# Gated DeltaNet in a fused decoder trunk: decay by selecting products, transposed A and attention, heads as a stair

## The chip, the cores and the metric

The kernel runs on one core of one Trainium2 chip. The metric is the device time of one execution in microseconds (us). TensorE (PE) multiplies matrices into PSUM, VectorE (DVE), ScalarE (ACT) and GpSimd (POOL) work on elements, and SyncE (SP) issues DMAs. Each engine takes its own instructions strictly in their order.

## What is computed

Two layers over 256 tokens with 1024 channels: a retention mixer with a SwiGLU, then a gated DeltaNet mixer with a SwiGLU, RMSNorm ahead of each and at the end. The change touches the DeltaNet mixer alone. It has 16 value heads and 8 key heads of 128 channels. The reference computes it in chunks of 64 tokens; both kernels use two chunks of 128, which is the same function.

```python
def rmsnorm(x, gain):
    xf = x.astype(jnp.float32)
    y = xf * lax.rsqrt(jnp.mean(xf * xf, axis=-1, keepdims=True) + NORM_EPS)
    return (y * gain.astype(jnp.float32)).astype(x.dtype)
...
def gated_delta_chunked(q, k, v, g, beta):
    """Gated delta rule S_t = a_t (I - b_t k_t k_t^T) S_{t-1} + b_t k_t v_t^T, o_t = S_t^T q_t."""
    ...
    gcum = jnp.cumsum(gc, axis=-1)
    ...
    decay_mat = jnp.where(causal, jnp.exp(gdiff), 0.0)
    k_beta = kc * bc[..., None]
    a_mat = jnp.where(strict, jnp.einsum('bhncd,bhnmd->bhncm', k_beta, kc) * decay_mat, 0.0)
    lhs = a_mat + jnp.eye(c, dtype=jnp.float32)
    rhs = jnp.concatenate([vc * bc[..., None], k_beta * jnp.exp(gcum)[..., None]], axis=-1)
    sol = lax.linalg.triangular_solve(lhs, rhs, left_side=True, lower=True, unit_diagonal=True)
    ...
    attn = jnp.where(causal, jnp.einsum('bhncd,bhnmd->bhncm', qc, kc) * decay_mat, 0.0)
    q_dec = qc * jnp.exp(gcum)[..., None]
    ...
    def step(state, xs):
        ui, wi, qi, ki, ai, gl = xs
        v_new = ui - jnp.einsum('bhcd,bhdv->bhcv', wi, state)
        o = jnp.einsum('bhcd,bhdv->bhcv', qi, state) + jnp.einsum('bhcm,bhmv->bhcv', ai, v_new)
        state = state * jnp.exp(gl)[..., None, None] + jnp.einsum('bhcd,bhcv->bhdv', ki, v_new)
        return state, o
...
def gdn_mixer(hdn, w_in, conv_w, a_log, dt_bias, norm_gain, w_out):
    proj = hdn @ w_in
    ...
    qkv = jax.nn.silu(causal_depthwise_conv(qkv, conv_w))
    ...
    beta = jax.nn.sigmoid(beta_logit.astype(jnp.float32))
    g = -jnp.exp(a_log.astype(jnp.float32)) * jax.nn.softplus(
        a.astype(jnp.float32) + dt_bias.astype(jnp.float32))
    o = gated_delta_chunked(q, k, v, g, beta)
    o = o * lax.rsqrt(jnp.mean(o * o, axis=-1, keepdims=True) + NORM_EPS) * norm_gain.astype(jnp.float32)
    o = o.reshape(b, s, GDN_V) * jax.nn.silu(z.astype(jnp.float32))
    return o.astype(hdn.dtype) @ w_out

def reference(x, positions, ...):
    h = x
    for i in range(DEPTH):
        ...
        h = h + mix          # retention for i = 0, gated DeltaNet for i = 1
        h = h + swiglu(rmsnorm(h, norm_ffn[i]), ffn_w_in[i], ffn_w_out[i])
    return rmsnorm(h, norm_final)
```

## The kernel before

All products with weights go through slabs of 128x1024 elements: SP loads raw, ScalarE casts whi (line 131), VectorE subtracts wlo (line 133), TensorE multiplies three times, high by high, high by low and low by high (lines 139 to 141). raw, whi and wlo have three buffers each. The projections use four PSUM banks (pool mm), everything else on TensorE four others (pool ip, tiles ip and tp).

The layer is a list of jobs, one for each slab (gdn, from line 1016). Beside them run generators, spawned by the jobs and moved on by one step after each job. From this a scheduler makes the order of every engine; the order is fixed in the built kernel.

- gates (line 641) makes beta and the log decay g, and by decay (line 718) the matrix D for each chunk and head: VectorE and GpSimd multiply a strict triangle by g (line 699, in a high and a low part gmh and gml), TensorE sums it with the triangle Ur (line 722), ScalarE takes the exponential of 512 columns, four heads at once (line 723).
- taps (line 725) is the convolution over four tokens of a projected slab in PSUM: one ScalarE and three VectorE instructions (line 732) for each half, then a silu on ScalarE.
- amat (line 754) makes A, the keys' products with beta and D: chunk 0 on VectorE (line 786), chunk 1 on ScalarE and GpSimd (lines 781, 782). invert (line 792) sends A to memory and back as Ab, so that all 32x32 diagonal blocks lie in partitions, inverts them by 31 pairs of VectorE instructions pr and Vb (lines 821, 823), sends the result to memory and back as Vd and Vc (lines 828, 831), transposes it (Tc, line 841), and merges blocks to 64 and to 128 by TensorE products and ScalarE copies (lines 857 to 891), one chunk after the other.
- attn (line 895): products of queries and keys, a ScalarE copy kq, a GpSimd product with D (line 925), four transposes for each (line 200), a ScalarE copy back into D.
- inner (line 935) is done for each group hg of four heads, once the inverse and the attention are there: solve (line 946), du (line 968), the products with the state (line 960) and with the attention (line 954), the norm and the gate with z; then yh and yl, the input of the output projection w_out (line 331).

The input projection's slabs come in the order z0 k q z1 v0 z2 v1 v2 v3 z3. In w_out the first six slabs of one half of the columns come, then six of the other half.

## Time and profile before

| | |
|---|---|
| median of 3 runs | 869.85 us (869.81 to 870.68) |
| the profiled execution | 869.91 us, of which its span is 868.1 us |
| granted TensorE clock | 0.997 of full speed |
| busy in the span | PE 842.7 us (97%), DVE 555.1 (64%), ACT 451.2 (52%), POOL 57.1 (7%) |
| chain of work that ended last | PE 80%, DVE 11%, the rest 9% |

The DeltaNet layer lies between about 400 and 675 us of the span. A timeline row gives the start and the length of a stretch of equal instructions; TensorE's matmuls overlap, so what one costs is read from start to start, and the idle time that a row names is a little less than what the queue lost. VectorE's instructions overlap by some 0.08 us too.

### The profile page before, as it was taken

Reading aid. Unit: us, or ns where it says so; the run is one execution under the profiler, and the core shown is the slowest. Engines: PE = TensorE matmul, PEld = TensorE weight load, DVE = VectorE, ACT = ScalarE, POOL = GpSimd, SP = SyncE. Lnnn points to the kernel's source line nnn. Section 1 sums busy time; section 2 is a strip of 40 time slices with the busy share of each in tenths; the row PEclk is TensorE's granted clock in tenths of the full one; section 3 lists DMA queues with packets and bytes.
Section 4 is the critical chain, followed back from the end, with each engine's and each line's share of the span. In section 5 each row is a group of like instructions: output and inputs, shape, how many; then the busy total and the mean of one; then the engine's idle time right before and its main releaser. Section 6 shows DMA issues by size and latency. Waiting matters only on the chain.

```text
span 868.1 us, 12759 instructions
## 1 busy us (share of the span) xinstructions
PE 842.7 (97%) x4917; PEld 718.6 (83%) x4917; DVE 555.1 (64%) x829; ACT 451.2 (52%) x770; POOL 57.1 (7%) x56
## 2 busy tenths in 40 slices
PE   8999999999999999999999988999899999999996
PEld 7789987888888889886998877989788888889885
DVE  4787877655555555454889899854665555555453
ACT  4553235554444444344687745687845544444343
POOL 0000000000000000000217141000200000000000
PEclk9999999999999999999999999999999999999998
DMA  8576445556556555554554734732045656555552
GB/s 262 186 208 173 123 146 165 174 193 197 189 179 189 184 183 174 189 191 122 146 147 127 214 99 137 191 135 73 4 167 169 210 180 193 180 183 182 183 193 74
DMA packets 121902, 143.54 MB, mean 165 GB/s; under 512 B 14145, under 2 KB 67954, under 8 KB 121842
## 3 DMA queue, kind: packets, MB, share of 16 engines
q1 hardware_dynamic: 121666, 142.66, 52.9%
q8 instruction: 38, 0.62, 0.3%
q14 instruction: 22, 0.18, 0.1%
q10 hardware_dynamic: 144, 0.07, 0.0%
q0 software_dynamic: 32, 0.01, 0.0%
HBM read 140.62 MB, written 2.10 MB: 164 GB/s over the span
## 4 chain that ended last, share of the span: by engine, by line
PE 80%; DVE 11%; issue 3%; DMA 3%; ACT 3%; POOL 1%; SPq 0%; POOLq 0%; ACTq 0%; DVEq 0%
PE mm L140 24%; PE mm L141 24%; PE mm L139 24%; DVE wlo L133 3%; PE tp L200 3%; DVE cacc L732 2%; DVE pr L821 2%; DVE Vb L823 1%; PE ip L960 1%; DMA raw<-gdn_w_in 1%; PE ip L552 1%; ACT junk L992 1%; DMA h<-x 1%; PE ip L946 1%; PE ip L544 1%
## 5 line engine op out<-in xcount | busy, mean ns | idle before, releaser
L133 DVE TENSOR_TENSOR wlo<-raw,whi 128x1024 fp32r<-128x1024 f32 x260 | 319.6, 1230 | 232.3 <-ACT whi L131 230.3
L131 ACT CAST whi<-raw 128x1024 fp32r<-128x1024 f32 x260 | 273.2, 1052 | 303.3 <-PE mm L140 225.2
L139 PE MATMUL mm<-whi,xh 128*128 128x512 f32 (+1 forms) x576 | 220.0, 385 | 1.2 <-ACT xh L636 0.7
L140 PE MATMUL mm<-whi,xl 128*128 128x512 f32 (+1 forms) x576 | 219.7, 382 | 0.5 <-DVE xl L315 0.3
L141 PE MATMUL mm<-wlo,xh 128*128 128x512 f32 (+1 forms) x576 | 208.0, 382 | 1.2 <-DVE wlo L133 1.2
L141 PEld LDWEIGHTS mm<-wlo,xh 128*128 128x128 f32 x576 | 108.5, 189 | 22.5 <-DVE wlo L133 2.6
L139 PEld LDWEIGHTS mm<-whi,xh 128*128 128x128 f32 x576 | 108.9, 189 | 21.1 <-ACT whi L131 1.0
L140 PEld LDWEIGHTS mm<-whi,xl 128*128 128x128 f32 x576 | 108.9, 189 | 21.0 <-issue 0.7
L139 PE MATMUL mm<-xh,whi 128*128 128x256 f32 x384 | 111.1, 289 | 0.0
L140 PE MATMUL mm<-xh,wlo 128*128 128x256 f32 x384 | 109.6, 285 | 1.2 <-DVE wlo L133 1.2
L141 PE MATMUL mm<-xl,whi 128*128 128x256 f32 x384 | 109.1, 284 | 0.0
L140 PEld LDWEIGHTS mm<-xh,wlo 128*128 128x128 f32 x384 | 73.4, 191 | 3.3 <-DVE wlo L133 1.8
L139 PEld LDWEIGHTS mm<-xh,whi 128*128 128x128 f32 x384 | 73.4, 191 | 1.3 <-issue 0.5
L141 PEld LDWEIGHTS mm<-xl,whi 128*128 128x128 f32 x384 | 73.4, 191 | 0.3
L139 PE MATMUL mm<-whi,hh 128*128 128x512 f32 x176 | 69.8, 397 | 0.0
L140 PE MATMUL mm<-whi,hl 128*128 128x512 f32 x176 | 69.6, 396 | 0.0
L141 PE MATMUL mm<-wlo,hh 128*128 128x512 f32 x176 | 64.3, 396 | 0.0
L732 DVE SCALAR_TENSOR_TENSOR cacc<-mm,conv,cacc 128x253 f32<-128x253 f32 (+2 forms) x96 | 45.6, 510 | 8.0 <-ACT cacc L729 7.4
L139 PE MATMUL mm<-whi,yh 128*128 128x512 f32 x128 | 49.5, 394 | 1.0 <-ACT yh L314 1.0
L140 PE MATMUL mm<-whi,yl 128*128 128x512 f32 x128 | 50.4, 394 | 0.0
L141 PE MATMUL mm<-wlo,yh 128*128 128x512 f32 x128 | 49.2, 397 | 0.0
L141 PEld LDWEIGHTS mm<-wlo,hh 128*128 128x128 f32 x176 | 33.1, 188 | 8.1
(235 smaller groups left out, 876.8 us busy)
## 6 DMA issues: line engine op xcount, KB each, us to landing
raw<-ffn_w_in SPq DMA_DIRECT2D x88, 512.0 KB, 3.5
raw<-ret_w_in SPq DMA_DIRECT2D x48, 512.0 KB, 4.0
raw<-gdn_w_in SPq DMA_DIRECT2D x48, 512.0 KB, 4.0
raw<-ffn_w_out SPq DMA_DIRECT2D x44, 512.0 KB, 3.6
raw<-ret_w_out SPq DMA_DIRECT2D x16, 512.0 KB, 3.3
raw<-gdn_w_out SPq DMA_DIRECT2D x16, 512.0 KB, 3.6
h<-x SPq DMA_DIRECT2D x4, 256.0 KB, 6.4
out<-o SPq DMA_DIRECT2D x4, 256.0 KB, 2.3
```

What stands on the lines that cost most here:

```text
L131: nc.scalar.copy(hi, raw)
L133: lo_ = nc.vector.tensor_tensor(lo, raw, hi.bitcast(F32), ALU.subtract)
L139: t.matmul(out, lh, rh, start=first, stop=False)
L140: t.matmul(out, ll, rh, start=False, stop=False)
L141: self.last_mm = t.matmul(out, lh, rl, start=False, stop=last).ins
L200: self.nc.tensor.transpose(out, in_, self.ident[:n, :n])
L544: nc.tensor.matmul(sp[:, c0:c0 + S - i0], k[:, d, j * P:(j + 1) * P], q[:, d, i0:S], start=d == 0, stop=d == 1)
L552: nc.tensor.matmul(op, sT[:, t * P:(t + 1) * P], b["v"][0][:, h], start=True, stop=t == 0)
L732: self.nc.vector.scalar_tensor_tensor(acc[:, s:S], ps[:, 0:S - s], cw[:, i, blk:blk + 1], acc[:, s:S], ALU.mult, ALU.add)
L821: V.tensor_tensor(tmp, Vb[:, 0:n, i:i + 1].broadcast_to([P, n, m]), Ab[:, n:32, i].unsqueeze(1).broadcast_to([P, n, m]), ALU.mult)
L823: V.tensor_tensor(Vb[:, 0:n, n:32], Vb[:, 0:n, n:32], tmp, ALU.subtract)
L946: T.matmul(up[:, j], b["V"][c][:, 4 * hg + j], v[c][:, j], start=True, stop=True)
```

## The change

- Decay: the running sum of g is transposed (gcT). For each group of heads and chunk one product writes "never" (-1e30 above the diagonal) into a PSUM bank, and for each head a product of 32 rows selects that head's row of gcT and adds it (tile_position). An exponential for each head, with the negative running sum as its bias, makes D, now transposed and with exact zeros, so the selections on GpSimd go.
- A is made transposed, both chunks by VectorE from PSUM. The squares of the norms replace one of the two scalings by beta: v is scaled by the key's norm kn, and uu is multiplied by beta2 on VectorE.
- The attention is one VectorE product from PSUM into D; copies, GpSimd products and transposes go.
- The merges use the transposed A, and each step is written for both chunks in a row. Tc comes ahead of the copies into Vf.
- inner of group hg starts when group hg-1 has taken two steps. The slabs come in the order z0 k q z1 z2 z3 v0 v1 v2 v3, and w_out changes between its halves after every two slabs up to the sixth.

```diff
-    def out_proj(self, w, yT, nk, nxt, early=None):
+    def out_proj(self, w, yT, nk, nxt, early=()):
...
-        p0 = self.proj_tok(w, 0, 512, yT, nk, None, (early,) if early else (), (), first)
-        p1 = self.proj_tok(w, 512, 512, yT, nk, None, (early,) if early else (), (last,), second)
+        p0 = self.proj_tok(w, 0, 512, yT, nk, None, early, (), first)
+        p1 = self.proj_tok(w, 512, 512, yT, nk, None, early, (last,), second)
...
+        gp = self.psip()
+        T.matmul(gp[:, 0:P], g4.rearrange("p r x -> p (r x)"), Uc, start=True, stop=True)
+        gcT = self.t1("gcT", (P,))
+        V.tensor_copy(gcT, gp[:, 0:P])
...
         b["D"] = [self.big(f"D{c}") for c in range(NT)]
-        pend = []
-        for c in range(NT):
-            for hg in range(4):
-                hs = slice(hg * 4, hg * 4 + 4)
-                gm = [self.t2(n, dt=F32R) for n in ("gmh", "gml")]
-                for eng, x, y in zip((V, V if hg % 2 else G), gm, (gh.bitcast(F32), gl)):
-                    eng.tensor_tensor(x, slb, y[:, c, hs].unsqueeze(2).broadcast_to([P, 4, P]), ALU.mult)
-                pend.append((c, hs, gm))
-                if len(pend) == 3:
-                    self.decay(b, Ur, *pend.pop(0))
...
-        for x in pend:
-            self.decay(b, Ur, *x)
+        never, eye = self.t1("never", (P,), F32R), self.t1("eye", (P,), F32R)
+        V.tensor_scalar(never, self.SL, -1e30, None, ALU.mult)
+        V.tensor_copy(eye, self.ident)
+        for hg in range(4):
+            dp = [self.psip().rearrange("p (h i) -> p h i", h=4) for _ in range(NT)]
+            for x in dp:
+                T.matmul(x, eye, never.unsqueeze(1).broadcast_to([P, 4, P]), start=True, stop=False)
+            for j in range(4):
+                for c in range(NT):
+                    q = 2 * (hg % 2) + c
+                    r, n = slice(32 * q, 32 * q + 32), 32 * q + c * NH + 4 * hg + j
+                    T.matmul(dp[c][:, j], self.ident[r, n:n + 1].broadcast_to([32, P]), gcT[r], start=False, stop=j == 3,
+                             tile_position=(32 * q, 0))
+            for c in range(NT):
+                for j in range(4):
+                    h = 4 * hg + j
+                    b["exp"] = A_.activation(b["D"][c][:, h], dp[c][:, j], AF.Exp,
+                                             bias=negc[:, c * NH + h:c * NH + h + 1]).ins
+            yield
         b["decayed"] = True
-
-    def decay(self, b, Ur, c, hs, gm):
-        dp = self.psip()
-        for i, x in enumerate(gm):
-            self.nc.tensor.matmul(dp, Ur, x.rearrange("p h j -> p (h j)"), start=i == 0, stop=i == 1)
-        b["exp"] = self.nc.scalar.activation(b["D"][c][:, hs].rearrange("p h j -> p (h j)"), dp, AF.Exp).ins
...
-        V.tensor_scalar(rk, b["kss"][:, :, ks], EPS, None, ALU.add)
-        G.tensor_tensor(rk, rk, self.mhalf[:, 0:4].rearrange("p (t h) -> p t h", t=NT), ALU.pow)
...
+        V.tensor_scalar(k2, b["kss"][:, :, ks], EPS, None, ALU.add)
+        G.tensor_tensor(rk, k2, self.mhalf[:, 0:4].rearrange("p (t h) -> p t h", t=NT), ALU.pow)
...
+        V.tensor_tensor(b["kn"][:, :, ks], k2, rk, ALU.mult)
+        V.tensor_tensor(rk, rk, rk, ALU.mult)
...
+        V.tensor_tensor(w2(beta2), w2(b["beta"]), rk.unsqueeze(3).broadcast_to([P, NT, 2, 2]), ALU.mult)
...
-            if c >= 1:
-                kk = self.t2("kk")
-                for j in range(4):
-                    h = 4 * sl + j
-                    A_.activation(kk[:, j], pp[:, j // 2], AF.Copy, scale=beta2[:, c, h:h + 1])
-                G.tensor_tensor(b["A"][c][:, 4 * sl:4 * sl + 4], kk, b["D"][c][:, 4 * sl:4 * sl + 4], ALU.mult)
-                continue
             for j in range(4):
                 h = 4 * sl + j
                 V.scalar_tensor_tensor(b["A"][c][:, h], pp[:, j // 2], beta2[:, c, h:h + 1], b["D"][c][:, h],
...
-        for c in range(NT):
-            for hg in range(4):
-                dm = b["D"][c][:, hg * 4:hg * 4 + 4]
-                G.affine_select(dm, dm, [[0, 4], [-1, P]], ALU.is_ge, 0.0, base=0, channel_multiplier=1)
...
-                            Ab[:, n:32, i].unsqueeze(1).broadcast_to([P, n, m]), ALU.mult)
+                            Ab[:, i, n:32].unsqueeze(1).broadcast_to([P, n, m]), ALU.mult)
             V.tensor_tensor(Vb[:, 0:n, n:32], Vb[:, 0:n, n:32], tmp, ALU.subtract)
...
-        yield
-        yield
+        for _ in range(4):
+            yield
+        V.transpose(Tc.rearrange("p a b -> p (a b)"), Vc.rearrange("p a b -> p (a b)"))
         for c in range(NT):
             for q in range(4):
                 qs = slice(32 * q, 32 * q + 32)
                 V.tensor_copy(Vf[c][qs, :, qs], Vc[qs, c * NH:(c + 1) * NH, :])
-        V.transpose(Tc.rearrange("p a b -> p (a b)"), Vc.rearrange("p a b -> p (a b)"))
...
         for c in range(NT):
             hs = slice(c * NH, (c + 1) * NH)
+            X.append(self.t2("X", (NH, 32)))
             xp = [h32(self.psip()) for _ in blocks]
             for h in range(NH):
                 for (q, b0, b1), x in zip(blocks, xp):
-                    T.matmul(x[b0, h], Am[c][b1, h, b0], Vc[b1, c * NH + h], start=True, stop=True,
-                             tile_position=(32 * q + 32, 32 * q))
+                    T.matmul(x[b1, h], Am[c][b0, h, b1], Tc[b0, c * NH + h], start=True, stop=True,
+                             tile_position=(32 * q, 32 * q + 32))
             for (q, b0, b1), x in zip(blocks, xp):
-                A_.copy(X[b0], x[b0])
-            yield
+                A_.copy(X[c][b1], x[b1])
...
+        yield
+        for c in range(NT):
             vp = [h32(self.psip()) for _ in blocks]
             for h in range(NH):
                 for (q, b0, b1), x in zip(blocks, vp):
-                    T.matmul(x[b0, h], Tc[b0, c * NH + h], X[b0, h], start=True, stop=True,
-                             tile_position=(32 * q, 32 * q))
+                    T.matmul(x[b0, h], X[c][b1, h], Vc[b1, c * NH + h], start=True, stop=True,
+                             tile_position=(32 * q + 32, 32 * q))
...
-        pend = None
         for c in range(NT):
             cs = slice(c * P, (c + 1) * P)
             for hp in range(4):
-                at = self.t2("att")
                 pp = self.psip().rearrange("p (x j) -> p x j", j=P)
                 for j in range(2):
-                    T.matmul(pp[:, j], b["qT"][:, 2 * hp + j, cs], b["kT"][:, 2 * hp + j, cs], start=True, stop=True)
-                kq = self.t2("kq", (2, P))
-                nc.scalar.copy(kq, pp[:, 0:2])
-                G.tensor_tensor(at.rearrange("p (j w) x -> p j w x", w=2),
-                                b["D"][c][:, 4 * hp:4 * hp + 4].rearrange("p (j w) x -> p j w x", w=2),
-                                kq.unsqueeze(2).broadcast_to([P, 2, 2, P]), ALU.mult)
-                if pend:
-                    flush(*pend)
-                pend = (c, hp, at)
+                    T.matmul(pp[:, j], b["kT"][:, 2 * hp + j, cs], b["qT"][:, 2 * hp + j, cs], start=True, stop=True)
+                dv = b["D"][c][:, 4 * hp:4 * hp + 4].rearrange("p (j w) x -> p j w x", w=2)
+                V.tensor_tensor(dv, pp[:, 0:2].unsqueeze(2).broadcast_to([P, 2, 2, P]), dv, ALU.mult)
                 yield
-        flush(*pend)
         b["attended"] = True
...
+        yield
+
+        while not (b.get("inverted") and b.get("attended") and (hg == 0 or b["steps"].get(hg - 1, 0) >= 2)):
+            yield
+        for _ in self.chunks(b, hg, v):
+            b["steps"][hg] = b["steps"].get(hg, 0) + 1
+            yield
+
+    def chunks(self, b, hg, v):
...
             uu = self.t2("uu")
-            A_.copy(f4(uu), f4(up))
+            V.tensor_tensor(uu, up, b["beta2"][:, c, hs].unsqueeze(2).broadcast_to([P, 4, P]), ALU.mult)
...
-            V.scalar_tensor_tensor(v[1][:, j], kp[:, j], b["beg"][:, 4 * hg + j:4 * hg + j + 1], v[1][:, j],
+            V.scalar_tensor_tensor(v[1][:, j], kp[:, j], b["nege"][:, 4 * hg + j:4 * hg + j + 1], v[1][:, j],
...
             for t in range(NT):
-                for j in range(2):
-                    h = 4 * hg + 2 * sl + j
-                    A_.activation(v[t][:, 2 * sl + j], tp[:, j, t], AF.Copy, scale=b["beta1"][:, t, h:h + 1])
+                h = 2 * hg + sl
+                A_.activation(v[t][:, 2 * sl:2 * sl + 2], tp[:, :, t], AF.Copy, scale=b["kn"][:, t, h:h + 1])
...
-        for group in "z0 k q z1 v0 z2 v1 v2 v3 z3".split():
+        for group in "z0 k q z1 z2 z3 v0 v1 v2 v3".split():
...
-        self.out_proj(w_out, yT, 16, nxt, early=6)
+        self.out_proj(w_out, yT, 16, nxt, early=(2, 4, 6))
```

Three places show what the scheduler makes of it. TensorE, decay, before: gmh and gml are the two parts of the products with g, Ur the triangle, mm the projection of k beside it.

```order
L722 MATMUL ip_3656<-gmh_3605,Ur_3520 128x512
L141 MATMUL mm_3799<-xl_3339,whi_3778 128x256
L139 MATMUL mm_3799<-xh_3338,whi_3778 128x256
L140 MATMUL mm_3799<-xh_3338,wlo_3779 128x256
...
L722 MATMUL ip_3656<-gml_3606,Ur_3520 128x512
...
L722 MATMUL ip_3700<-gmh_3644,Ur_3520 128x512
L722 MATMUL ip_3700<-gml_3645,Ur_3520 128x512
```

The same place after; never and eye are the constant and its unit matrix, gcT the transposed running sum, cst the constants' tile that selects.

```order
L711 MATMUL ip_3522<-never_3518,eye_3519 128x512
L711 MATMUL ip_3523<-never_3518,eye_3519 128x512
L716 MATMUL ip_3522<-gcT_3498,cst_75 128x128
L716 MATMUL ip_3523<-gcT_3498,cst_75 128x128
...
L711 MATMUL ip_3566<-never_3518,eye_3519 128x512
L716 MATMUL ip_3566<-gcT_3498,cst_75 128x128 x4
L140 MATMUL mm_3847<-xh_3338,wlo_3766 128x256
```

Two products of 512 columns for each bank, spread among the projection, have become one of 512 and four of 128 in a block; the selecting ones alternate between two banks in one part (c of 0 and 1 at different rows), and go four at a time to one bank in another.

ScalarE after, in the middle of the v slabs; zs3 is the silu of the last z group from its banks mm_4696 and mm_4697, vc and cacc the convolution of v. Before, z3 was the last group and stood behind all v slabs.

```order
L131 CAST whi_5449<-raw_5448 128x1024
L738 ACTIVATE vc_5255<-cacc_5262 128x256
L730 ACTIVATE cacc_5387<-mm_5321,conv_86 128x256
L131 CAST whi_5509<-raw_5508 128x1024
L1038 ACTIVATE zs3_3423<-mm_4696 128x512
L1038 ACTIVATE zs3_3423<-mm_4697 128x512
L131 CAST whi_5554<-raw_5553 128x1024
```

The two silus stand behind the cast of the slab whi_5509, five v slabs' casts and more behind the end of z3 itself.

TensorE, last head groups, before: Vf is the inverse, D the attention, numbers of uu and v tell the groups.

```order
L954 MATMUL ip_5919<-uu_5876,D1_3526 128x128 x4
L954 MATMUL ip_5925<-uu_5883,D1_3526 128x128 x4
L954 MATMUL ip_5931<-uu_5890,D1_3526 128x128 x4
L946 MATMUL ip_5937<-v_5594,Vf0_4973 128x128 x4
L960 MATMUL ip_6030<-du_5944,kn0_3417 128x256 x2
L954 MATMUL ip_6034<-uu_5942,D0_3525 128x128 x4
```

The same part after, up to the first product of w_out (mm_5916).

```order
L941 MATMUL ip_5559<-uu_5519,D1_3517 128x128 x4
L933 MATMUL ip_5565<-v_5253,Vf0_4772 128x128 x4
L947 MATMUL ip_5640<-du_5572,kn0_3417 128x256 x2
L941 MATMUL ip_5644<-uu_5570,D0_3516 128x128 x4
...
L200 MATMUL tp_5766<-cst_75,v_4851 128x128 x4
L933 MATMUL ip_5773<-v_5253,Vf1_4773 128x128 x4
...
L139 MATMUL mm_5916<-whi_5813,yh_5757 128x512
```

Before, three groups go side by side and the fourth follows them; after, each group follows the one ahead, and the first slab of w_out stands behind the first group's output and the second group's solve.

## Rows read from the trace of the kernel before

**Rows 1.** the page, part 1: engine busy us (share of the span) xinstructions

```profile
PE 842.7 (97%) x4917; PEld 718.6 (83%) x4917; DVE 555.1 (64%) x829; ACT 451.2 (52%) x770; POOL 57.1 (7%) x56
```

**Rows 2.** windows: length, busy us of PE, PEld, DVE, ACT, POOL, clock, DMA

```profile
450.00:500.00 50.00, 47.94 (x351) 44.26 (x351) 45.74 (x94) 38.28 (x119) 21.82 (x19) 1.00 0.61 165
500.00:550.00 50.00, 44.01 (x314) 39.96 (x314) 49.27 (x89) 26.18 (x50) 12.33 (x7) 1.00 0.49 140
550.00:600.00 50.00, 49.02 (x674) 44.71 (x674) 30.10 (x49) 36.79 (x77) 0.00 (x0) 1.00 0.46 136
600.00:650.00 50.00, 46.72 (x264) 40.04 (x263) 31.06 (x79) 34.75 (x110) 6.54 (x4) 1.00 0.22 73
```

**Rows 3.** PE's waits, 400 to 640: us in total, times, longest

```profile
PE tp L200 <- POOL att L925: 2.7, 3, 1.7
PE tp L200 <- ACT vc L737: 2.1, 2, 1.2
PE ip L960 <- DVE du L968: 2.0, 1, 2.0
PE mm L140 <- DVE wlo L133: 1.2, 1, 1.2
PE mm L141 <- DVE wlo L133: 1.2, 1, 1.2
PE mm L139 <- ACT yh L314: 1.0, 1, 1.0
```

**Rows 4.** PE timeline: start us, us, engine, line, operation, count, [idle before <-releaser]

```profile
437.46 0.39 PE L722 MATMUL ip<-gmh,Ur 128*128 128x512 f32 x1
437.69 0.40 PE L722 MATMUL ip<-gml,Ur 128*128 128x512 f32 x1
...
506.25 0.66 PE L200 MATMUL tp<-cst,att 128*128 128x128 f32 x4 [1.73 <-POOL att L925]
506.74 0.61 PE L922 MATMUL ip<-kT,qT 128*128 128x128 f32 x4
...
555.17 1.20 PE L857 MATMUL ip<-Vc,A 32*32 32x32 f32 x64 [0.39 <-DMA Vc<-Vd]
556.30 0.39 PE L141 MATMUL mm<-xl,whi 128*128 128x256 f32 x1
...
561.00 1.08 PE L872 MATMUL tp<-Tc,X 32*32 32x32 f32 x29
...
609.75 2.84 PE L954 MATMUL ip<-uu,D 128*128 128x128 f32 x24
612.43 1.06 PE L946 MATMUL ip<-v,Vf 128*128 128x128 f32 x8
```

**Rows 5.** VectorE timeline, inside the recurrence and at its end

```profile
502.28 0.58 DVE L821 TENSOR_TENSOR pr<-Vb,Ab 128x220 f32<-128x220 f32 x1
502.77 0.48 DVE L732 SCALAR_TENSOR_TENSOR cacc<-mm,conv,cacc 128x255 f32<-128x255 f32 x1
503.17 0.38 DVE L823 TENSOR_TENSOR Vb<-Vb,pr 128x220 f32<-128x220 f32 x1
...
503.85 1.22 DVE L133 TENSOR_TENSOR wlo<-raw,whi 128x1024 fp32r<-128x1024 f32 x1
504.99 1.63 DVE L821 TENSOR_TENSOR pr<-Vb,Ab 128x231 f32<-128x231 f32 x1
...
555.06 3.44 DVE L840 COPY Vf<-Vc 32x512 f32<-32x512 f32 x8 [2.86 <-DMA Vc<-Vd]
558.52 1.25 DVE L841 STREAM_TRANSPOSE Tc<-Vc 128x1024 f32<-128x1024 f32 x1
```

**Rows 6.** DMA queue of SP, timeline: the round trips of A and of V

```profile
475.77 4.09 SPq L805 DMA_DIRECT2D Ad<-A  x8
...
546.04 0.34 SPq L828 DMA_DIRECT2D Vd<-Vb  x1
```

**Rows 7.** tile pr, 487 to 492: ns min/median/max, first and last start, forms

```profile
L821 DVE TENSOR_TENSOR pr<-Vb,Ab x3: 209/259/309, 488.2 to 491.8; 128x31 f32<-128x31 f32 x1, 128x60 f32<-128x60 f32 x1, 128x87 f32<-128x87 f32 x1
```

**Rows 8.** groups by line, 400 to 625: out<-in, shapes, count, busy us, mean ns

```profile
L968 DVE TENSOR_TENSOR du<-uu,dec 128x512 f32<-128x512 f32 x4 | 2.8, 692 | 3.5 <-ACT uu L948 3.5
```

102 lines of the change are left out of this document (43 added, 59 removed).

## The prediction

> **What bounds the kernel now.** I read the page's busy shares first, then a table of windows along the span, then TensorE's waits, and last the timelines of the stretch that stood out. TensorE is busy 842.7 us of 868.1 [rows 1], so the time is TensorE's queue plus its stops, and the question is where it stops. The windows show it: of 200 us from 450 to 650 it is idle for 2.1 us in the first 50, 6.0 in the second, 1.0 in the third and 3.3 in the last [rows 2]. So some 12 us are to be won by removing stops, all in this layer. The waits name them: 2.7 us for the attention product of GpSimd (line 925), 2.1 us for ScalarE's convolved v, 1.2 us for the low half of a weight slab (wlo) from VectorE at line 140 and, in a second row alike, at line 141, then 2.0 us for the state's input du and 1.0 us for yh at the start of w_out [rows 3]. In the 500 to 550 window VectorE is busy 49.3 of 50 us [rows 2]: there it sets the pace, and whatever waits for wlo, taps or v waits for VectorE.
>
> VectorE's own rows say why it is so full there. A product of 220 columns takes 0.58 us, one of 231 columns right behind it 1.63 us [rows 5] while GpSimd was at its line 925, whose end released TensorE at 506.25 [rows 4]. Summed over all such rows between 485 and 553, against the same shapes with GpSimd idle, it is about 7 us. The change takes nearly all large work from GpSimd, so those 7 us go; but it hands VectorE new work in the same place.
>
> **The change part by part: TensorE's queue.** Out go 16 decay products of 512 columns, one each 0.235 us (437.46 to 437.69, and the next alike) [rows 4], 3.8 us, and 32 attention transposes, four in 0.49 us (506.25 to 506.74) [rows 4], 3.9 us. In come eight 512-column products with the constant "never", 1.9 us, and 32 selecting products of 128 columns. These are full float32, for which the trace shows two records a product, 24 records in 2.68 us (609.75 to 612.43) [rows 4], so 0.223 us each: 7.1 us if they run one after the other. No row shows 32-row tiles with 128 columns. The nearest are the merges: line 857, alternating between two tiles, needs (1.20-0.19)/64 = 16 ns a record (0.19 us is the length of one), line 872, on one tile, (1.08-0.19)/28 = 32 ns [rows 4]. By that ratio the 18 selecting products that stand in alternation (the order shows them) take half, 2.0 us less: 5.1 us. The gates' new small product and transpose I put at 0.4 us. A change between tiles of 32 rows and the full array showed about 0.1 us (last record of the line 857 group begins at 556.18, line 141 at 556.30) [rows 4]; the new decay has 12 such changes, 0 to 1.2 us. Sum: -3.8-3.9+1.9+0.4 plus 5.1 to 7.1 plus 0 to 1.2, that is -0.3 to +2.9; nothing decides between the ends, and I take **+1.5 us**.
>
> A page's rule weighs on that last price. The Trainium skill, TensorEngine Tiling (Array Packing), Key Properties, states that changing the tiling mode drains TensorE. The row here shows 0.1 us for it; with the full length of a record, 0.39 us in that row, 12 changes would be 4.7 us instead of 1.2.
>
> **The chain through VectorE.** Between the last element of A and the transposed inverse Tc stands one chain: A goes to memory and back (issue 475.77 [rows 6], first pr at 488.2 [rows 7]: 12.4 us), the recurrence of 31 pairs pr and Vb runs in VectorE's queue until Vd is issued at 546.04 [rows 6] (57.8 us), V goes to memory and back until 555.06, and Tc ends at 559.77 [rows 5]: 84.0 us in all. The new order lets me count VectorE's queue between first pr and last Vb: 31 pairs, 22.5 us (a pair of 220 columns takes 0.49 for pr and 0.30 for Vb, start to start [rows 5]; scaled by columns); 17 wlo at 1.14 (503.85 to 504.99), 19.4; 30 taps at 0.40 (502.77 to 503.17) [rows 5], 11.9; 8 attention products at 0.69, the price of du's 512 columns [rows 8], 5.5; three small ones 0.3. That is 59.6 us and no idle time, against 57.8 before: the lengthening that goes is eaten by the attention products and by more slabs and taps. Tc now comes ahead of the Vf copies, whose eight took 3.44 us [rows 5]. New chain: 12.4+59.6+9.0+1.25 = 82.3 us, 1.7 shorter.
>
> What TensorE has to do meanwhile, from its new order: 142 products of 512 columns at 0.235, 309 of 256 columns at 0.12, half of that, 16 float32 products at 0.223 and 10 transposes at 0.12: 75.2 us. So at least 7.1 us of stops remain before the merges. A second thing adds to it: the order leaves z3's two silu copies on ScalarE until behind the cast whi_5509, and until then they hold two of the four PSUM banks that projections use. Three v slabs in a row then start only when VectorE has done the taps of the slab two before; played through by hand with the prices above, TensorE reaches the merges 8 to 9.5 us late instead of 7.1. Against that stand 9.0 us of stops between 450 and 600 now [rows 2]. The attention's waits go, the wait for wlo and banks takes their place. I take 8.0, **-1.0 us**; ends 6 (-3.0: the banks come free in time and two slabs of lead are in hand) and 10.5 (+1.5: the k and q slabs stop too).
>
> **Merges, heads and the output projection.** The merges have as many products as before; in lockstep, one chunk's products stand while the other's copies run, and I see no stop above the 0.1 us of now. The heads are different. Before, three groups of heads go through their state step side by side: line 954 shows 24 records in a row, three groups [rows 4], so each group's copy is covered by two others' products. The fourth alone has the wait of 2.0 us for du [rows 3]. Now group hg starts when hg-1 is two steps on, since v3 ends the input projection and w_out needs y0 at once. In the order, TensorE's du product of the second group waits for a VectorE multiply that stands behind taps of v, which wait for ScalarE's queue of squares and v copies: 1.5 to 3 us. uu is now a VectorE multiply with beta2 (0.69 us [rows 8]) that TensorE waits for twice uncovered, about 0.9 us each. y0's start takes the 1.0 us for yh as before, y3's perhaps once more. I get about 5.1 us for 3.3 now [rows 2]: **+1.8 us**, with ends 0 (the alternating columns of w_out cover all of it, as nearly now) and +6 (all three following groups pay du's 2.0 us).
>
> **Edits at nothing.** ScalarE loses the kq, attention, kk and uu copies and gains 24 smaller exponentials: it is busy 38.3 of 50 us at its fullest [rows 2] and nobody waits for it in the decay unless it falls behind four banks, about 1 us. GpSimd's powers stay. The earlier table load stands between casts at the layer's entry: 0 to 1.3 us, taken as 0. The other layers are the same instructions.
>
> **Sum.** 1.5-1.0+1.8 = +2.3 us on the profiled execution's 869.91, 0.06 above the median: **872.1 us**. A measurement of this kernel can tell 0.2%, 1.7 us, from no change, so this is just over that line.
>
> **Rivals.** First, faster: VectorE free of GpSimd gets ahead. If the bank wait doesn't come, the stops before the merges fall to 6 (-3.0), the paired selecting products cost -0.3 and the heads cost half of my price less 0.4 (+0.5): 869.9-2.8 = about 867; with the heads at no cost, 866.5. For it speaks the 7 us of lengthening that go; against it that the recurrence's queue counts 59.6 us without any. It decides from a recurrence below some 57 us. Second, much slower: the stair of heads, three waits of 2.0 us for du, +6 instead of +1.8, with the rest 876.3, and 878 with the upper price of TensorE's queue. For it speaks that one lone group paid it before; against it that w_out's slabs lie between the later groups. Third, the drain at each change of tile, 12 times 0.39 us [rows 4] in place of the 0.6 in my sum: 876.2. Against it stands the 0.1 us worked out from the same row. The page named above has this rule.
>
> **How the numbers follow.** The forecast's case, stops change places, 0.50, with its own range 868.5 to 875.5: 0.02 of it faster, 0.26 within 0.2%, 0.22 slower. VectorE ahead 0.27, all faster. Stair of heads 0.15, slower. Drain 0.08, of that 0.02 within. Faster 0.29, same 0.28, slower 0.43. For eight in ten the range takes the forecast's case and most of both neighbours: down to 864.5, where the lowest ends of chain and queue meet (-3.0, -0.3, and the entry's two waits gone), up to 878.5.
>
> **What would show it.** Right: no line of TensorE waiting for an attention product; between 485 and 555 VectorE still busy above 95%, no pr over 0.7 us; TensorE's waits there for wlo and for taps (PSUM banks) of v, 6 to 8 us in all; first pr to Vd's issue 58 to 61 us; a stop of 1.5 us or more before the second group's du product; selecting products 0.11 us apart a record, or half that in alternation. Wrong: a recurrence under 57 us, TensorE idle below 2 us between 500 and 550, selecting products far above 0.25 us each, or stops in the decay, for which I have put nothing.

## The result, and the profile after

The changed kernel takes 879.60 us (median of 4 runs, 879.11 to 880.97) against 869.83 us (868.21 to 870.68) before: a ratio of 1.0111, with a 95% interval from 1.0093 to 1.013. It is slower, by four times what was forecast, and above the range. The profiled execution is 880.0 us with a span of 878.2, so 10.1 us above the profiled execution of before.

The page answers to [rows 1]: TensorE's busy time has grown by 12.1 us, while VectorE, ScalarE and GpSimd have all become lighter. The second line is the clock granted to TensorE in 40 slices, in tenths.

```profile
PE 854.8 (97%) x4944; PEld 730.9 (83%) x4944; DVE 544.1 (62%) x853; ACT 441.4 (50%) x738; POOL 26.7 (3%) x32
...
PEclk9999999999999999999969999989999999999999
```

The next fence has the windows that answer to [rows 2], with the one from 400 to 450 besides (length, busy us of PE, PEld, DVE, ACT, POOL with counts, clock, DMA share, GB/s).

```profile
400.00:450.00 50.00, 47.24 (x295) 39.60 (x294) 25.85 (x52) 25.05 (x58) 0.54 (x1) 0.89 0.43 117
450.00:500.00 50.00, 50.00 (x367) 47.74 (x367) 38.14 (x93) 35.55 (x99) 7.55 (x6) 0.97 0.58 156
500.00:550.00 50.00, 47.11 (x299) 42.97 (x298) 47.16 (x102) 26.05 (x50) 2.97 (x1) 0.97 0.59 159
550.00:600.00 50.00, 48.77 (x699) 47.62 (x698) 28.89 (x51) 31.19 (x51) 0.00 (x0) 0.93 0.46 128
600.00:650.00 50.00, 46.87 (x266) 40.82 (x265) 36.34 (x84) 35.20 (x109) 4.91 (x3) 0.97 0.22 76
```

The row of before that [rows 2] does not have, from the same view:

```profile
400.00:450.00 50.00, 48.70 (x343) 43.84 (x341) 38.51 (x67) 31.91 (x63) 7.32 (x6) 1.00 0.48 131
```

Read two columns of it. **Idle time**: over these 250 us TensorE was idle for 13.6 us before (250 less 48.70 and the four of [rows 2]) and is idle for 10.0 now. So the stops in these windows became 3.6 us fewer. **The clock**: it was 1.00 in all five windows and is now 0.89, 0.97, 0.97, 0.93 and 0.97. The missing shares, 0.11+0.03+0.03+0.07+0.03 of 50 us, come to 13.5 us.

Cut finer, the missing share sits in four places. In each the clock is at 0.50, the lower of its two levels (1.2 instead of 2.4 GHz).

```profile
434.00:438.00 4.00, 4.00 (x35) 3.10 (x34) 2.73 (x9) 2.75 (x11) 0.00 (x0) 1.00 0.49 131
438.00:440.00 2.00, 2.00 (x12) 1.57 (x11) 1.10 (x3) 2.00 (x9) 0.00 (x0) 0.73 0.00 0
440.00:452.00 12.00, 12.00 (x56) 9.80 (x56) 1.56 (x2) 6.30 (x22) 0.00 (x0) 0.50 0.17 46
...
537.00:540.00 3.00, 0.30 (x3) 0.09 (x1) 3.00 (x8) 1.04 (x1) 0.00 (x0) 1.00 0.83 229
...
542.00:544.00 2.00, 2.00 (x11) 2.00 (x11) 1.93 (x7) 0.78 (x2) 0.00 (x0) 0.50 0.46 138
...
568.00:574.00 6.00, 6.00 (x245) 5.83 (x238) 5.53 (x10) 5.83 (x9) 0.00 (x0) 1.00 0.24 55
...
576.00:582.00 6.00, 6.00 (x55) 5.71 (x51) 1.44 (x3) 3.29 (x7) 0.00 (x0) 0.50 0.52 175
...
610.00:612.00 2.00, 2.00 (x11) 2.00 (x11) 1.96 (x7) 1.71 (x4) 0.45 (x1) 0.50 0.00 0
```

With the part windows at their edges they last 13.7, 3.4, 6.8 and 3.4 us, 27.3 in all. The second and the fourth follow stops of TensorE (busy 0.30 of 3.00 from 537 to 540; the stops before 610 are below). The first and the third do not: TensorE's records fill every microsecond before the clock falls (the profile models where a product ends, so short gaps inside a record can't be ruled out). Ahead of 438 they are the new selecting products, ahead of 574 the merges of both chunks.

TensorE's timeline (start, length, engine, line, operation, count, idle before it in brackets) shows what half clock costs, and places to which the points below return.

```profile
435.06 1.16 PE L716 MATMUL ip<-gcT,cst 32*128 32x128 f32 x16
436.15 0.49 PE L711 MATMUL ip<-never,eye 128*128 128x512 f32 x1
436.57 1.15 PE L716 MATMUL ip<-gcT,cst 32*128 32x128 f32 x8
437.65 0.39 PE L140 MATMUL mm<-xh,wlo 128*128 128x256 f32 x1
...
440.17 0.41 PE L140 MATMUL mm<-xh,wlo 128*128 128x256 f32 x1
440.38 0.41 PE L141 MATMUL mm<-xl,whi 128*128 128x256 f32 x1
...
447.67 2.08 PE L716 MATMUL ip<-gcT,cst 32*128 32x128 f32 x16
449.68 0.58 PE L141 MATMUL mm<-xl,whi 128*128 128x256 f32 x1
...
452.73 0.28 PE L140 MATMUL mm<-xh,wlo 128*128 128x256 f32 x1
452.85 0.28 PE L141 MATMUL mm<-xl,whi 128*128 128x256 f32 x1
...
567.77 2.21 PE L844 MATMUL ip<-Tc,A 32*32 32x32 f32 x128
...
608.60 1.10 PE L947 MATMUL ip<-du,kn 128*128 128x256 f32 x4 [1.97 <-DVE f L977]
...
668.48 0.96 PE L139 MATMUL mm<-whi,yh 128*128 128x512 f32 x3 [0.73 <-ACT yh L314]
669.82 0.50 PE L140 MATMUL mm<-whi,yl 128*128 128x512 f32 x1 [0.37 <-DVE yl L315]
```

A product of 256 columns takes 0.21 us from start to start at 440 and 0.12 at 452.7, so the half clock costs 0.09 of each 0.21 us, 43%. Of 27.3 us that is 11.7; by the missing shares, which count half of the time as lost, it is 13.5.

The balance of the 10.1 us goes by the page. TensorE's busy time grew by 12.1 us, and its idle time fell by 2.0, from 25.4 (868.1 less 842.7) to 23.4 (878.2 less 854.8). That is less than the 3.6 of the windows, because 1.5 us of new stops lie behind 650: 0.73 for yh and 0.37 for yl of the last group of heads (668.48 and 669.82 above), and 0.4 more for the input of the SwiGLU that follows. Of the 12.1 us of busy time the clock takes 11.7 by the first price and more than all by the second. So TensorE's longer queue is left with 0.4 us at most, where 1.5 had been put.

Its waits from 400 to 660 answer to [rows 3]: us in total, times, longest.

```profile
PE mm L139 <- DVE cacc L733: 4.1, 2, 2.9
PE mm L139 <- ACT xh L636: 2.1, 1, 2.1
PE ip L947 <- DVE f L977: 2.0, 1, 2.0
PE ip L941 <- DVE uu L935: 1.0, 1, 1.0
```

The attention's 2.7, the convolution's 2.1 and the two waits for wlo have gone; the wait for yh has moved behind this window, to the last group. The product at 608.60 reads du, which ends at 608.45 (VectorE's row further down); f, which the table names, only ended last. The taps of v (cacc) that free a PSUM bank are new.

### The profile page after: what moved, and what is told of

Same layout as the page of the kernel before. It is cut to its first block, busy times and chain, and to the rows that moved or that the text cites. A ratio compares the mean times of both kernels' runs of the same rounds, so it can differ in the third digit from the quotient of the medians.

```text
span 878.2 us, 12767 instructions
## 1 busy us (share of the span) xinstructions
PE 854.8 (97%) x4944; PEld 730.9 (83%) x4944; DVE 544.1 (62%) x853; ACT 441.4 (50%) x738; POOL 26.7 (3%) x32
## 4 chain that ended last, share of the span: by engine, by line
PE 90%; DVE 2%; ACT 2%; DMA 2%; issue 2%; SPq 0%; POOL 0%; POOLq 0%; ACTq 0%
PE mm L141 26%; PE mm L140 26%; PE mm L139 26%; PE tp L200 3%; DMA raw<-ret_w_in 2%; PE ip L716 1%; DVE wlo L133 1%; PE ip L947 1%; PE ip L941 1%; PE ip L552 1%; ACT whi L131 1%; PE ip L544 1%; DVE cacc L733 0%; PE ip L872 0%; PE ip L882 0%
## 5 line engine op out<-in xcount | busy, mean ns | idle before, releaser
L139 PEld LDWEIGHTS mm<-whi,xh 128*128 128x128 f32 x576 | 108.7, 189 | 23.9 <-ACT xh L636 2.4
L139 PE MATMUL mm<-xh,whi 128*128 128x256 f32 x384 | 113.3, 295 | 4.1 <-DVE cacc L733 4.1
L141 PE MATMUL mm<-xl,whi 128*128 128x256 f32 x384 | 111.9, 291 | 0.0
L140 PE MATMUL mm<-xh,wlo 128*128 128x256 f32 x384 | 111.5, 290 | 0.0
L139 PEld LDWEIGHTS mm<-xh,whi 128*128 128x128 f32 x384 | 75.7, 197 | 5.7 <-issue 3.5
L140 PEld LDWEIGHTS mm<-xh,wlo 128*128 128x128 f32 x384 | 75.8, 197 | 1.3 <-issue 1.0
L141 PEld LDWEIGHTS mm<-xl,whi 128*128 128x128 f32 x384 | 75.8, 197 | 0.6 <-issue 0.4
L733 DVE SCALAR_TENSOR_TENSOR cacc<-mm,conv,cacc 128x255 f32<-128x255 f32 (+2 forms) x96 | 44.8, 477 | 25.7 <-ACT cacc L730 24.8
```

The costliest lines, as they stand in the source:

```text
L139: t.matmul(out, lh, rh, start=first, stop=False)
L140: t.matmul(out, ll, rh, start=False, stop=False)
L141: self.last_mm = t.matmul(out, lh, rl, start=False, stop=last).ins
L733: self.nc.vector.scalar_tensor_tensor(acc[:, s:S], ps[:, 0:S - s], cw[:, i, blk:blk + 1], acc[:, s:S], ALU.mult, ALU.add)
```

## The experiments

The theory from this reading: the 32-row selecting products and the merges in lockstep bring the clock down by themselves, and without them the kernel would be a little faster than before. The rival: the lower clock is a trait of the denser layer, or comes from stops, and moves elsewhere when these products change.

**Selecting products on all 128 rows.** The same number of products and columns, without small tiles. The order is nearly the same: two products of the projection come between the last groups.

```diff
-                    q = 2 * (hg % 2) + c
-                    r, n = slice(32 * q, 32 * q + 32), 32 * q + c * NH + 4 * hg + j
-                    T.matmul(dp[c][:, j], self.ident[r, n:n + 1].broadcast_to([32, P]), gcT[r], start=False, stop=j == 3,
-                             tile_position=(32 * q, 0))
+                    n = c * NH + 4 * hg + j
+                    T.matmul(dp[c][:, j], self.ident[:, n:n + 1].broadcast_to([P, P]), gcT, start=False, stop=j == 3)
```

> After, with the 32 selecting products on all 128 rows (the transposed running sum lies there four times, so the selector is a full column of the unit matrix and no tile position is given). Same number of products and columns. Theory clock by rows: the granted clock fell to 0.50 from 438.9 to 453.4 in after because the products there use a quarter of the array's rows; then this fall is gone, and of its 13.7 us half, some 6 to 7 us, come back: 872.5 to 874. Two products can no longer run side by side, which costs 1 to 2 us of that. Rival, the fall comes from waiting (blocks paced by the exponentials, many small float32 products), whatever rows they use: still a fall there, 879 to 881. Rival, the clock costs nothing because TensorE waits there anyway: the fall goes and the time stays within 1 us of 879.6.

880.99 us (879.89 to 882.61), ratio 1.0123 (1.0101 to 1.0146). The time is missed, the place is right. The windows of this kernel show the decay at full clock, and the merges at half for longer than after:

```profile
436.00:454.00 18.00, 18.00 (x153) 17.75 (x152) 7.36 (x15) 16.75 (x51) 0.00 (x0) 1.00 0.19 54
560.00:566.00 6.00, 6.00 (x190) 5.83 (x184) 3.16 (x4) 4.29 (x8) 0.00 (x0) 1.00 0.46 128
...
568.00:588.00 20.00, 20.00 (x163) 19.14 (x161) 5.20 (x10) 10.42 (x20) 0.00 (x0) 0.50 0.08 28
```

So the 32 rows of the selecting products are what costs the clock in this decay. In the merges, whose code is the same, 6.8 us at half became 23.9: how long a fall lasts is not fixed by the stretch that sets it off. With three falls of 3.4 us behind stops (402, 535 and 610) this kernel is at half for 34.1 us, 6.8 more than the changed one, so what the decay gave back was lost again.

**Merges chunk by chunk**, four steps for one chunk, then four for the other, as before; the rest as after.

```diff
-        for c in range(NT):
+        for cc in range(NT):
+            for c in (cc,):
...
-        yield
+            yield
```

> After, with the merges of one chunk following the other as in before (eight steps instead of four), all else as in after. Theory clock by small tiles in one block: the fall from 575 to 583 (both chunks' 32x32 products close together) is gone, the others stay, 3 us less, about 876 to 877, if the later start of the heads doesn't take it back. Rival, the merges' fall is set by the waits around them: it stays, 879 to 881.

880.54 us in a single run. The decay's fall is there as in the changed kernel (0.50 from 440 to 451), the merges are at 1.00 throughout, and two falls of 3.4 and 6.8 us come with stops of 3.05 and 4.25 us (a stop's length is given from start to start of the products around it, less the 0.12 us of one product). The place is right again, and again the time stays: the longer stop, for du, has a fall of its own.

**Both edits together.**

> Both edits: selecting products on all rows, merges one chunk after the other. Theory clock: only the two short falls near 541 and 610 are left, each 3.4 us long; 869 to 871.5. Rival, falls come from waits: clock as in after, 878 to 882.

873.41 us (870.95 to 875.12, 10 runs) where before took 870.84 beside it: ratio 1.0028 (1.0014 to 1.0042). This takes some 7 of the 10 us back. In its profile the clock is 0.97, 1.00, 0.97, 1.00 and 1.00 in the five windows: the decay and the merges are whole, and what remains in the layer are 3.4 us behind the entry's stop and 3.4 behind the stop for a PSUM bank. The theory holds for most of the loss, but the 869 to 871.5 us that it gave are missed by 2, and this kernel is not faster than before.

**The small products alone, in the kernel before.** 32 selecting products of 32 rows, which nobody reads, are added behind the decay.

```diff
+        for hg in range(4):
+            dp = [self.psip().rearrange("p (h i) -> p h i", h=4) for _ in range(NT)]
+            for j in range(4):
+                for c in range(NT):
+                    q = 2 * (hg % 2) + c
+                    r, n = slice(32 * q, 32 * q + 32), 32 * q + c * NH + 4 * hg + j
+                    T.matmul(dp[c][:, j], self.ident[r, n:n + 1].broadcast_to([32, P]), self.U[r], start=True, stop=True,
+                             tile_position=(32 * q, 0))
```

> The kernel before, with 32 selecting products of 32 rows and 128 columns added at the end of its decay, on the triangle's rows, into PSUM banks that nobody reads; its result is that of before. It measures these products alone. One after the other they cost 7.1 us, side by side 4 to 5: 874 to 877 without a fall of the clock. Theory clock by rows: the granted clock falls there and the time is 2 to 7 us above that, 877 to 883. Rival, no fall: 874 to 877 and a clock of 0.997 as in before.

879.44 us in a single run, and the clock stays at 1.00 from 440 to 452, around these products. Here 60 of the 64 records stand in two blocks among products of the projection; in the changed kernel they alternate with the "never" products. They also read another operand and alternate between two tiles throughout (57 ns a record in the longer block), where 16 records of the changed kernel go on one tile right ahead of its fall. Which of these differences keeps the clock was not tested. So small tiles do not bring the clock down wherever they stand, and this run does not support the theory, though its time lies in the theory's range. Its 9.5 us over the profiled execution of before come from elsewhere: some 4 of products, 2.4 more idle time between 400 and 650 (16.0 for 13.6), and two falls of 3.4 us, at 563 and 624, which were not in the kernel before.

**Lockstep merges alone, in the kernel before.**

```diff
+        X, T2, X2 = [], [], []
         for c in range(NT):
-            X = self.t2("X", (NH, 32))
+            X.append(self.t2("X", (NH, 32)))
...
-            yield
+        yield
+        for c in range(NT):
             vp = [h32(self.psip()) for _ in blocks]
```

> The kernel before with nothing but both chunks' merges in lockstep, four steps for eight. Theory, the 32x32 products close together bring the clock down by themselves: a fall of the granted clock inside the merges, 871 to 874. Rival, they do so only behind the new decay or beside v slabs that wait: clock 0.994 or more, 868 to 871.

871.98 us in a single run, 869.22 before beside it. The merges lose the clock here too:

```profile
556.00:558.00 2.00, 0.89 (x56) 0.78 (x49) 1.95 (x5) 0.60 (x1) 0.00 (x0) 0.77 0.89 319
558.00:566.00 8.00, 6.25 (x80) 6.09 (x81) 6.21 (x10) 7.24 (x14) 0.00 (x0) 0.50 0.39 119
```

The clock is low for 10.2 us. All three kernels with lockstep merges lose it for 6.8 us or more there. Of the ten other kernels, before among them, four show one fall of 3.4 us in or near their merges and six none. But in this one a wait of 2.5 us for Tc stands in the same window, so it does not separate the products from the stop.

**What is left over: entry, slab order, banks and stair.** Five kernels build on the two edits together. The first undoes the order of the slabs and of the heads:

```diff
+        yield
...
-        while not (b.get("inverted") and b.get("attended") and (hg == 0 or b["steps"].get(hg - 1, 0) >= 2)):
+        while not (b.get("inverted") and b.get("attended")):
...
-        for group in "z0 k q z1 z2 z3 v0 v1 v2 v3".split():
+        for group in "z0 k q z1 v0 z2 v1 v2 v3 z3".split():
...
-        self.out_proj(w_out, yT, 16, nxt, early=(2, 4, 6))
+        self.out_proj(w_out, yT, 16, nxt, early=(6,))
```

> The arithmetic of after (decay by selecting products, A and attention by VectorE from PSUM, uu by VectorE) with full-row selecting products and the order of before: slabs z0 k q z1 v0 z2 v1 v2 v3 z3, w_out in sixes, merges chunk by chunk, heads without the stair, and the gates' first step given back, so that ScalarE's table load at the layer's entry stands behind the casts of xh again. Theory, the time is TensorE's queue, its stops and half of its time at the half clock, and the order of slabs brought the stops at 537 and 553 (PSUM banks held by z3): no such stops, no fall of the clock before the end; 864 to 867, below before. Rival, VectorE is as full as before and its wlo come as late whatever the order: 868 to 872.

875.44 us (875.11 to 876.42), ratio 1.0057 (1.0041 to 1.0074). Both times are missed, the rival's by 3.4 us. The stops for taps and banks grow, from 4.3 us in the kernel with both edits to 5.9, plus 1.8 for a silu of z, and the clock falls three times for 3.4 us (from 536, 553 and 573). On the order the rival was right: the new slab order is not what makes these stops.

The second only gives the gates' generator its step back, behind the copy of ba:

```diff
         V.tensor_copy(ba, ps)
+        yield
```

> The third experiment (full rows, merges apart) with the gates' first step given back. Theory: TensorE's stop at the layer's entry is 0.9 us again instead of 2.3 and the short fall of the clock at 404 goes: 1.4 to 3 us less than 873.4, 870 to 872. Rival, the entry's stop comes from the two xh casts and not from the table load: 872 to 875.

870.97 us in a single run, 871.07 before. The wait for xh at the entry is 0.7 us again instead of 2.1. Two variants of it, without the stair of heads and with the stair but the old slab order, each in a single run:

> As the run with full rows, merges apart and the entry, but each group of heads starts as soon as the inverse and the attention are there, as in before; slabs still end with v3. Theory, the stair's uncovered waits for du (2.0, 1.2, 0.7 us in the third experiment) cost 2 us: 869 to 871. Rival, without z3's slabs behind v3 nothing covers the last group in either way: no change against the run beside it, within 1 us.

875.67 us.

> The first of these four with the stair of heads kept: tells the stair apart from the order of slabs. Theory, the order of slabs is what counts: 865 to 868, within 1.5 us of the first. Rival, the stair costs by itself: 3 us or more above it.

872.96 us. Neither expectation came as it was put. TensorE's stops of over 1.3 us in the layer come to 11.2 and 9.7 us, for 8.4 in the kernel that they vary. Seven later runs of that kernel (below) have a median of 873.42 us, so without the stair it is 2.3 us slower, and with the old slab order the same. The old order shows it a second time: with the stair it is 2.5 us faster than the 875.44 without. So the stair seems to save some 2 us in either order, and the order of slabs moves the time by 0.5 us or less; single runs, which can be off by as much as the stair saves, say no more. The fourth holds back the casts of later slabs until z's silu is done, so that the banks come free:

```diff
-        nc.scalar.copy(hi, raw)
+        with self.tc.issue_after(self.zlast) if self.zlast else ExitStack():
+            nc.scalar.copy(hi, raw)
...
-                        A_.activation(zv(t), ps[t], AF.Silu)
+                        self.zlast = A_.activation(zv(t), ps[t], AF.Silu).ins
```

> The run with full rows, merges apart and the entry, with one more tie: no later cast of a slab may be ordered ahead of the silu of a finished z group, so z3's two PSUM banks come free right behind its slabs. The scheduler then orders other things anew too: the merges stand two v slabs earlier, ahead of their taps. Theory, the stop of 3.0 us at 529 comes from the banks: no wait of a projection for taps of more than 2 us, and no fall of the clock near 533; 866 to 869. Rival, the banks are not what is late, the recurrence is: TensorE waits 6 us or more for Vc or Tc instead, 872 to 878.

877.61 us in a single run. The waits for banks go, and TensorE waits for one slab's wlo instead, 11.6 us at a stretch, until 534.1. In VectorE's queue that wlo stands behind the last pairs of the recurrence, which end at 532.8. So the rival's time came, and the recurrence is what was late, though TensorE met it at wlo and not at Vc or Tc.

The kernel with the gates' step again, in seven runs:

> The run with full rows, merges apart and the gates' first step again, timed against before. One look gave 870.97 beside a before of 871.07. Theory, without the falls in decay and merges the change is worth nothing by itself: 869 to 872, within 0.2% of before. Rival, some falls of the clock come and go between executions and the median is 2 us or more above.

873.42 us (872.41 to 874.38), 870.48 before, ratio 1.0038 (1.0025 to 1.005). The rival held, and the single run had been a lucky one. The two profiles of this same kernel show with what: first the earlier one, around the stop for du, then the later one.

```profile
589.00:593.50 4.50, 0.69 (x6) 0.53 (x5) 2.84 (x6) 1.51 (x4) 0.00 (x0) 1.00 0.08 31
593.50:600.00 6.50, 6.50 (x45) 6.09 (x45) 4.80 (x12) 5.88 (x21) 0.00 (x0) 1.00 0.01 3
```

```profile
592.00:594.00 2.00, 0.07 (x1) 0.10 (x1) 2.00 (x5) 0.00 (x0) 0.00 (x0) 0.59 0.00 0
594.00:598.00 4.00, 4.00 (x15) 3.63 (x16) 1.62 (x4) 1.76 (x4) 0.00 (x0) 0.50 0.02 4
```

The stop is 4.0 us in both; once the clock stays, once it is at half for 6.8 us.

**The stop for du taken away.** du is made straight from PSUM with beta2 times the decay, ahead of uu, instead of from uu:

```diff
-        def solve(c):
+        def solve(c, du=None):
...
+            if du is not None:
+                bd = self.ph.tile([P, 4], F32, name="bd", bufs=2)
+                V.tensor_tensor(bd, b["beta2"][:, 0, hs], b["dec"][:, hs], ALU.mult)
+                V.tensor_tensor(du, up, bd.unsqueeze(2).broadcast_to([P, 4, P]), ALU.mult)
...
-        u0 = solve(0)
...
-        V.tensor_tensor(du, u0, b["dec"][:, hs].unsqueeze(2).broadcast_to([P, 4, P]), ALU.mult)
+        u0 = solve(0, du)
```

> The kernel beside it, with du made straight from the PSUM bank of the solve, by beta2 times dec, ahead of uu, instead of from uu: same products, one VectorE multiply less in front of TensorE's next product for each group. Theory, du stands behind taps that wait for ScalarE: the stop of 4.0 us at 589 falls by the 0.7 us of one multiply and the tap between them, 1 us at most, and the others by as much: 1 to 2 us less than beside it, 868.5 to 870. Rival, only the taps' wait counts, and du comes as late: same within 0.7 us.

867.03 us (866.12 to 868.19, 10 runs), 870.48 before, ratio 0.9961 (0.995 to 0.9971): faster than before and than the changed kernel. The expectation had put 1 to 2 us; it is 6.4 less than the kernel beside it. Its wait for du is 0.95 us where the kernel without this edit waited 3.8, so 2.9 less, where 1 at most had been put:

```profile
589.86 1.10 PE L951 MATMUL ip<-du,kn 128*128 128x256 f32 x4 [0.95 <-DVE du L937]
```

At least a part of the rest lies in the order of VectorE's queue: du now stands ahead of a tap that it stood behind, and that tap had waited 1.66 us for ScalarE. The clock is whole in every window of the layer, as [rows 2] had it before. TensorE is idle for 8.1 us between 400 and 650, where before had 13.6.

```profile
500.00:550.00 50.00, 45.25 (x320) 42.10 (x319) 48.26 (x104) 25.79 (x51) 2.98 (x1) 1.00 0.60 170
550.00:600.00 50.00, 48.85 (x708) 46.59 (x708) 32.26 (x60) 36.66 (x77) 0.00 (x0) 1.00 0.37 106
```

Its page gives what TensorE's queue costs without a fall, 843.3 us where before has 842.7 [rows 1]:

```profile
PE 843.3 (98%) x4944; PEld 720.4 (83%) x4944; DVE 543.3 (63%) x857; ACT 439.7 (51%) x738; POOL 27.6 (3%) x32
```

Between the two profiled executions lie 7.7 us (874.22 and 866.56): the shorter wait is 2.9 of them, and the clock, 10.2 us at half in the one and none in the other, 4.4 to 5.1 by the two prices above. One part of that is not explained by the edit: the 3.4 us at half near 534 come ahead of du in time, behind a stop of 3.0 us, and the faster kernel has a stop of 3.4 at the same place and keeps its clock.

## Why the prediction was wrong

**The step that failed has no term in the sum.** The prediction counted TensorE's time as its queue plus its stops, priced every product by rows at full clock, and wrote "stops in the decay, for which I have put nothing" among what would make it wrong. No stop came in the decay, but 13.7 us at 1.2 GHz did. The profile of before could not show it: its clock was 1.00 in all windows [rows 2], and its only blocks of 32-row tiles were the merges, chunk by chunk. What it did show is that the change puts small tiles at two places where none, or half as many in a row, had stood, and that the clock is a condition for every price. A case could have been set beside the others: the block of the new decay is some 10 us long at full clock (434.87 to 445.27 in the first experiment; 434.42 to 449.68 here), and at half clock the products measured here take 1.8 to 1.9 times as long (0.21 for 0.12 us; 126 for 68 ns a record, by 447.67 to 449.68 and 435.06 to 436.15), so a fall over all of that block costs 8 to 9 us, an estimate from these rows.

What the runs show of the cause: in the new decay it is the 32 rows of the selecting products (13.7 us at half in both kernels with 32 rows, none in all eight with 128 rows). For the merges the lockstep is what the three kernels with the long falls share, and going back to chunks took them away; that it is the products and not the stops around them is shown only where no stop stood ahead (the changed kernel and the one with 128 rows). Why the same 32-row products kept the clock in the kernel before stays open. The Trainium skill, TensorE: Matmul & The Clock Gate, HAM oscillation — how this bites in real kernels, puts such losses down to gaps in which TensorE waits. The trace agrees at 541, behind 2.9 us of waiting, and speaks of more at 438 and 574, where TensorE was busy 4.00 us of the 4.00 and 6.00 of the 6.00 ahead.

**TensorE's queue, +1.5.** The balance leaves 0.4 us at most, and the last experiment's page, without a fall, shows 0.6 (843.3 for 842.7). That is inside the term's -0.3 to +2.9, but a third of what was taken. The alternating products do run side by side: 16 records in 1.09 us (435.06 to 436.15), 68 ns each, against 56 expected; those on one tile need 135 ns (1.08 us for 8, 436.57 to 437.65), more than the 112 taken. On 128 rows, in the first experiment and in the last, a record needs 100 ns (0.81 us for 8). So both prices were too low, and other parts of the term too high; which ones was not taken apart. The drain at each change of tile, rival three, did not come at its size. From a "never" product to the small ones behind it is 0.42 us (436.15 to 436.57), and on 128 rows, where no tile changes, it is 0.31 at the same place:

```profile
437.11 0.47 PE L711 MATMUL ip<-never,eye 128*128 128x512 f32 x1
437.42 1.05 PE L715 MATMUL ip<-gcT,cst 128*128 128x128 f32 x8
438.23 0.36 PE L140 MATMUL mm<-xh,wlo 128*128 128x256 f32 x1
```

So a change costs 0.1 us, the price that the prediction had taken from its row, and not 0.39.

**The chain through VectorE, -1.0.** Its mechanism was right and its size too small. The next three fences are SP's DMA issues, VectorE's tile pr (count, shortest, median and longest ns, first and last start), and VectorE's timeline, of the changed kernel.

```profile
486.31 4.20 SPq L798 DMA_DIRECT2D Ad<-A  x8
...
556.42 0.36 SPq L817 DMA_DIRECT2D Vd<-Vb  x1
```

```profile
L810 DVE TENSOR_TENSOR pr<-Vb,Ab x31: 183/360/426, 498.9 to 555.9; 128x31 f32<-128x31 f32 x2, 128x60 f32<-128x60 f32 x2, 128x87 f32<-128x87 f32 x2, 128x112 f32<-128x112 f32 x2
```

```profile
565.70 1.25 DVE L826 STREAM_TRANSPOSE Tc<-Vc 128x1024 f32<-128x1024 f32 x1 [2.72 <-DMA Vc<-Vd]
...
605.40 0.48 DVE L733 SCALAR_TENSOR_TENSOR cacc<-mm,conv,cacc 128x255 f32<-128x255 f32 x1 [0.88 <-ACT cacc L730]
...
606.39 0.47 DVE L733 SCALAR_TENSOR_TENSOR cacc<-mm,conv,cacc 128x254 f32<-128x254 f32 x1
606.78 0.68 DVE L935 TENSOR_TENSOR uu<-ip,beta 128x512 f32<-128x512 f32 x1
...
607.77 0.68 DVE L952 TENSOR_TENSOR du<-uu,dec 128x512 f32<-128x512 f32 x1
```

The longest pr is 0.43 us; the 1.63 of [rows 5] is gone with GpSimd's work. From the first pr to Vd's issue it is 57.5 us (forecast 59.6, before 57.8), from A's issue to the end of Tc 80.6 (forecast 82.3, before 84.0). TensorE's idle time between 450 and 600 is 4.1 us, all of it at the PSUM banks; waits for banks and for wlo had been forecast, 8.0 in all, and 9.0 was there before [rows 2]. So this term is -4.9 instead of -1.0. VectorE is busy for 54.4 of the 57.5 us, so its queue was shorter than the 59.6 counted, and not without gaps. The shorter chain is 1.7 of the difference; the rest was not taken apart. That z3's silus hold two banks is in ScalarE's timeline:

```profile
400.38 1.28 ACT L664 ACT_TABLE_LOAD   x1
...
558.75 1.08 ACT L1038 ACTIVATE zs<-mm 128x512 f32<-128x512 f32 x2
```

They run at 558.75, behind both stops for banks (from 537 and from 553).

The first rival, VectorE ahead, was thus nearer to the stops than the forecast was: by the balance, which no run shows by itself, the changed kernel would stand some 1.5 us below before without the clock's loss. Its condition, a recurrence under 57 us, did not come by half a microsecond. The last experiment's kernel, at 867.03, has just the time that rival named, with other edits in it; that is luck and does not bear the rival out.

**The heads, +1.8.** The wait for du of the second group came where it was put, behind taps that wait for ScalarE (0.88 us at 605.40, then uu and du between taps), and cost 2.0 us. uu cost 1.0 once, not 0.9 twice. The wait for yh went from the first group to the last, which the prediction had as a "perhaps", and cost 0.73 there with 0.37 for yl. By the windows the idle time from 600 to 650 is 3.1 us for 3.3; with the 1.1 at 668 the term is +1.0. The second rival, three full waits, did not come, and the two pairs of kernels above speak for the stair as a gain and not a cost.

**The entry, taken at 0.** The table load stands at 400.38 on ScalarE, ahead of xh's casts, and TensorE's wait for xh went from 0.7 to 2.1 us. The upper end, 1.3, was right.

**The sum.** By windows and waits: -4.9 for the chain, +1.0 for the heads, +1.4 for the entry and +0.4 behind the mixer make -2.1 of idle time (2.0 by the page's rounded figures), where -1.0+1.8+0 stood. With 0.4 for the queue the forecast's own terms, sized as measured, give about 868, 4 us below the forecast; the clock's 11.7 make it 880. So with these terms alone the kernel would have come out a little faster than before, and the term that was missing made it slower.

## What to carry to other kernels

A price read at full clock holds only while the clock is full: where a change makes a stretch of TensorE denser in small tiles, add a case in which that stretch runs at 1.2 GHz, and price it from rows. Look at the granted clock by windows before any wait, since a busy TensorE at half clock looks like a longer queue. Work that is moved off a wait is worth more than the wait where the stop also takes the clock: here the edit that removed 2.9 us of waiting came with 6.4 us between the medians, of which a part is not explained by it.

## What was not expected of the hardware

- Behind selecting products of 32 rows and 128 columns the clock was at half for 13.7 us, with no idle time in the records ahead; the same products on 128 rows kept it, and were quicker than the unpaired ones (100 for 135 ns a record). Products of the same shape in other surroundings, in the kernel before, kept it too.
- The clock's falls are not the same from one execution to the next. The 17 longest stops in the DeltaNet layer of these kernels last 3.0 to 11.7 us, and 14 of them have a fall in them or within 1.5 us behind them; three, of 3.0, 3.4 and 4.0 us, have none, and the last is of a kernel that fell at the same place in another execution. Shorter stops, of 2.1 to 2.4 us, went both ways. Six of the fourteen profiles also have a fall of 3.4 us near 8 us, where all kernels run the same instructions; before and the changed kernel have none there.
- Half clock did not double TensorE's time: 0.21 for 0.12 us, a product of 256 columns.
